# Attention probabilities and a first set of folded weights: their multiplications by VectorE in place of GpSimd

## The chip, the cores and the metric

The kernel runs on one core of a Trainium2 chip. The metric is the device time of one execution in microseconds (us): the median of several runs. The profile describes one execution, instruction by instruction. Engines are TensorE (PE in the profile, its weight loads PEld), VectorE (DVE), ScalarE (ACT), GpSimd (POOL) and SyncE (SP, which issues most of the DMAs).

## The reference, cut to what matters

Two small transformer stacks run one after the other on 512 tokens of width 1024, in float32. The change touches their two self-attentions. The first, with a forget gate, has 16 heads of 64 features and a causal mask; the norm's gain `kv_norm_g` stands ahead of the keys and values:

```
hk = rmsnorm(x, kv_norm_g);  kvf = hk @ kvf_w          # keys, values, gate
q  = rmsnorm(x, norm_mix_g[1]) @ fox_wq
s  = q @ k.T / 8 + (c_q - c_k);  s = where(key <= query, s, -inf)
p  = softmax(s);  out = (p @ v) @ fox_wo
```

The second is a sum of three dilated branches, which the kernel computes as one softmax over 512 keys with a bias table (the number of branches that hold a key, and the relative bias, stand in it), again with 16 heads of 64:

```
q, k, v = split(rms_norm(x, mix_norm[1]) @ w_qkv)
o = softmax(q @ k.T / 8 + bias + log(count)) @ v;  x = x + o @ w_out
```

Around them lie a convolution block, two cross-attentions to 256 memory tokens, two squared-ReLU MLPs, a short convolution and two SwiGLU MLPs.

## The kernel before, in words

All activations lie transposed, 128 features on the partitions and 512 tokens along the row, in 8 tiles. A float32 product is made of three TensorE products of rounded parts: each operand is split into a high part (`whi`, `ahi`; ScalarE rounds it, lines 770, 215) and a remainder (`wlo`, `alo`; VectorE subtracts, lines 773, 216), and `mm3` (line 171) adds high x high, high x remainder and remainder x high into one PSUM bank.

Both attentions run `heads_attention` (line 735). Heads go in pairs, since two heads of 64 fill 128 partitions. For each pair, `KeysQueries` loads the weight columns of its keys and queries into one raw tile; `parts_of` (line 755) cuts them into pieces, and each piece is a chain: `gained` multiplies the raw weights in place by the norm's gain, one factor per row (line 760, in the first attention alone, where three projections with two gains read one activation), `high` rounds them, `low` makes the remainder. These chains are put on a list and issued one step at a time between matmuls (`tick`). Values are projected in four groups of 256 columns (`v_steps`), their weights cut in the same way. In a piece's owner, `owner[1]` is the number of the pair or of the value group, so `owner[1] > 0` leaves out the first pair's keys and queries (four multiplications) and the first group of values (four). The other 40 are given to a function `pinned`.

When a pair's key and query products end, `evac` (line 799) scales them (line 801), ScalarE rounds them (806), and VectorE makes the remainders (808) and a copy (814) that the scores read; GpSimd clears halves of a tile (812).

`scores(head)` (line 939) makes four tiles of scores, one per block of 128 queries; block i has (i + 1) x 128 keys, so the tiles have 512, 384, 128 and 256 columns in the order 3, 2, 0, 1. For each tile VectorE adds the bias and takes the row's extreme (line 967), ScalarE takes the exponential and the row's sum (970), VectorE the reciprocal of the sum (971), and GpSimd multiplies the tile by it (972). In the first attention the bias itself is made by ScalarE (1188) and masked by GpSimd (1191) for up to three tiles of a head ahead of time. `transposed` (line 976) then transposes the four tiles by TensorE (`transpose`, line 93), ten blocks, into PSUM, where they are split in two parts; `values` multiplies them with the values one part of a head later (`pend`).

Between the scores of a head and its transposes, and between those and the next head, other matmuls fill the time of TensorE: the next pair's keys and queries, the values, the output projection. `PLAN`, `PLAN_AHEAD` and `FRACS` say how many. So the tiles of probabilities have a fixed amount of TensorE work in which to become ready.

The order on each engine is made by the framework when the program is built: it simulates the program with costs of its own, and gives an engine that is free in that simulation the earliest line that is ready. TensorE's matmuls, and what goes through `pinned`, keep the order of the program among themselves on their engine. Each engine then executes its list strictly in that order.

Of the kernel before, what the change touches and what calls it, by code (L numbers as in the profile page):

```python
# [13 lines left out]
OP = mybir.AluOpType  # L14
AX = mybir.AxisListType

P = 128
# [63 lines left out]
def model_kernel(tc, a, c_mats, c_onehot, c_lnn, out):  # L81
    nc = tc.nc
# [6 lines left out]
    def matmul(*args, **kw):  # L89
        tc.keep_in_program_order(nc.tensor.matmul(*args, **kw))  # L90
# [4 lines left out]
    def pinned(ins):  # L95
        return tc.keep_in_program_order(ins)
# [20 lines left out]
    def bank(tag="g"):  # L117
        return psum["pool"].tile([P, 512], F32, name="ps_" + tag, tag=tag, bufs=psum["bufs"][tag])
# [616 lines left out]
    def heads_attention(specs, fold, h, nrm, bias_of, hp, wo, prologue, ahead=0):  # L735
# [19 lines left out]
        def parts_of(owner, view, nk, width, f, cuts, pl, tag):  # L755

            w = []

            def gained(v, k0, n):
                ins = nc.gpsimd.tensor_tensor(  # L760
                    v, v, f[:, k0 : k0 + n].unsqueeze(2).to_broadcast([P, n, width]), op=OP.mult
                )
                if owner[1] > 0:
                    pinned(ins)

            def high(v, k0, n):
                if not w:
                    w.append(pl.tile([P, nk, width], F32R, name="whi", tag="whi" + tag, bufs=2))
                    w.append(pl.tile([P, nk, width], F32R, name="wlo", tag="wlo" + tag, bufs=2))
                nc.scalar.copy(w[0][:, k0 : k0 + n, :], v)  # L770

            def low(v, k0, n):
                nc.vector.tensor_tensor(  # L773
                    w[1][:, k0 : k0 + n, :], v, w[0][:, k0 : k0 + n, :].bitcast(F32), op=OP.subtract
                )

            n = nk // cuts
            for k0 in range(0, nk, n):
                v = view[:, k0 : k0 + n, :]
                for fn in (gained, high, low) if f is not None else (high, low):  # L780
                    pieces.append((owner, lambda fn=fn, v=v, k0=k0: fn(v, k0, n)))
            return w
# [148 lines left out]
        def bias_early(head):  # L931

            if head not in biases:
                biases[head] = {}
                bias_fns[head] = bias_of(head)
            i = (3, 2, 0, 1)[len(biases[head])]
            biases[head][i] = bias_fns[head](i)

        def scores(head):
            pair, e = divmod(head, 2)  # L940
            sm = hp.tile([P, NT], F32, name="sm", tag="sm", bufs=3)
            mx = hp.tile([P, NT], F32, name="mx", tag="mx", bufs=3)
            rs = hp.tile([P, NT], F32, name="rs", tag="rs", bufs=3)
            sall = hp.tile([P, 10 * P], F32, name="sall", tag="s", bufs=1)
            pr = [None] * NT
            half = None
            parts = []
            for i in (3, 2, 0, 1):
                n = (i + 1) * P
                if i == 0:  # L950
                    sc = half[:, 3 * P :]
                else:
                    sc = bank("s")
                    if i == 2:
                        half = sc
                    sc = sc[:, 0:n]
                qq = qk[pair][1][0][:, e, i * P : (i + 1) * P]
                matmul(sc, qq, qk[pair][0][0][:, e, 0:n], start=True, stop=False)
                matmul(sc, qq, qk[pair][0][1][:, e, 0:n], start=False, stop=True)
                parts.append((i, sc))  # L960
            for n, (i, sc) in enumerate(parts):
                if n + BIAS_AHEAD < NT:
                    bias_early(head)
                elif head < 15:
                    bias_early(head + 1)
                s = sall[:, P * i * (i + 1) // 2 : P * (i + 1) * (i + 2) // 2]
                nc.vector.tensor_tensor_reduce(
                    s, sc, biases[head][i], 1.0, 3.0e38, op0=OP.add, op1=OP.min, accum_out=mx[:, i : i + 1]
                )
                nc.scalar.activation(s, s, AF.Exp, scale=-1.0, bias=mx[:, i : i + 1], accum_out=sm[:, i : i + 1])  # L970
                nc.vector.reciprocal(rs[:, i : i + 1], sm[:, i : i + 1])  # L971
                pinned(nc.gpsimd.tensor_scalar(s, s, rs[:, i : i + 1], 1.0, op0=OP.mult, op1=OP.mult))  # L972
                pr[i] = s
            return pr

# [79 lines left out]
        for pair in range(8):  # L1055
            n, late = (PLAN_AHEAD if ahead else PLAN)[pair]
            seq = [lambda: stream_run(1)] * (n - late)
            if pair < 7:
                seq = seq + [lambda pair=pair: kq_run(pair + 1, 1)] * 16
            seq = seq + [lambda: stream_run(1)] * late  # L1060
            total = len(seq)
            done = 0
            for e in range(2):
                head = pair * 2 + e
                pr = scores(head)
                fr = (FIRST_FRACS if head == 0 else FRACS) if pair < 7 else LAST_FRACS
                for part in range(3):
                    goal = int(round(total * (e + sum(fr[: part + 1])) / 2))
                    for fn in seq[done:goal]:
                        fn()  # L1070
                    done = goal
                    if part == 0 and pend is not None:
                        values(*pend)
                        pend = None
                    if part == 1:
                        pend = (head, transposed(pr))
# [343 lines left out]
```

## Time and profile before

| | |
|---|---|
| median of 3 runs | 2662.1 us (2660.45 to 2663.39) |
| the profiled execution, and its span | 2659.51 us, 2657.7 us |
| TensorE busy | 2605.3 us, 98% of the span |
| VectorE busy | 1489.1 us, 56% |
| ScalarE busy | 1096.9 us, 41% |
| GpSimd busy | 555.0 us, 21% |
| line 972 on GpSimd, 128 products | 75.9 us, 604 ns on average |
| line 760 on GpSimd, 48 multiplications | 53.9 us, 1147 ns on average |
| mean granted clock of TensorE | 0.994 |

The span is the time from the first to the last instruction; the execution's own time holds some 1.8 us more around it. [...] A wait is listed with the engine that waited and the instruction whose end released it last. In a row of the timeline, brackets hold the idle time of that engine ahead of the instruction; a row without them followed the one before it without idle time.

### The profile page before, as it was taken

The page shows a single profiled execution, that of the slowest core. Times are in us where ns is not written, and L with a number is a line of the kernel's source. Part 1 is how long each engine was busy: PE and PEld are TensorE (multiplying, and loading weights), DVE is VectorE, ACT ScalarE, POOL GpSimd, SP SyncE. Part 2 cuts the span into 40 slices and gives each one's busy share as a digit, 9 for nine tenths or more (in the row PEclk, how much of TensorE's full clock was granted, in tenths as well). Part 3 has the DMA queues.
Part 4 walks back from the last instruction along what each step waited for, and adds up shares of the span by engine and source line. Part 5 has one row for each costly group of instructions (what it writes and reads, how often), then busy time and mean ns, then how long its engine had stood idle before and what let it go on. Part 6 is the DMA issues. An engine that isn't in the chain of part 4 may idle for free.

```text
span 2657.7 us, 32286 instructions
## 1 busy us (share of the span) xinstructions
PE 2605.3 (98%) x12521; PEld 2184.0 (82%) x12521; DVE 1489.1 (56%) x2215; ACT 1096.9 (41%) x1843; POOL 555.0 (21%) x586
## 2 busy tenths in 40 slices
PE   8999999999999999999999999999999999999999
PEld 6889888888878877888888788878888888788888
DVE  6995664443558887554344665343335777643333
ACT  6755443322337665442223323232224666422223
POOL 5862120000226532110000501111112221210111
PEclk9999999999999999999999999999999999999999
DMA  7255133233322322233333233843323323233331
GB/s 211 83 197 181 48 111 95 95 95 95 96 77 68 100 76 72 78 105 103 102 97 95 80 95 97 114 142 102 100 86 111 92 84 90 76 96 99 95 87 56
DMA packets 318057, 264.82 MB, mean 100 GB/s; under 512 B 6741, under 2 KB 304273, under 8 KB 317905
## 3 DMA queue, kind: packets, MB, share of 16 engines
q1 hardware_dynamic: 313808, 252.90, 31.3%
q0 software_dynamic: 1616, 5.52, 1.9%
q10 hardware_dynamic: 2480, 4.33, 0.5%
q8 instruction: 99, 1.62, 0.2%
q14 instruction: 54, 0.43, 0.0%
HBM read 251.16 MB, written 11.57 MB: 99 GB/s over the span
## 4 chain that ended last, share of the span: by engine, by line
PE 56%; DVE 2%; DMA 2%; issue 1%; ACT 1%; POOL 0%; ACTq 0%; DVEq 0%; POOLq 0%
PE ps_g L90 52%; DMA raw<-in_ffn_w_gate 2%; PE ps_s L90 2%; PE ps_t L90 1%; PE ps_t L93 1%; DVE wlo L168 0%; DVE x L1261 0%; DVE alo L228 0%; POOL ssq L252 0%; DVE x L574 0%; ACT ahi L227 0%; DVE x L1259 0%; DVE x L916 0%; ACT sq L248 0%; DVE wlo L773 0%
## 5 line engine op out<-in xcount | busy, mean ns | idle before, releaser
L90 PE MATMUL ps_g<-ahi,whi 128*128 128x512 f32 x3052 | 1196.5, 392 | 9.2 <-DVE x L574 4.9
L90 PE MATMUL ps_g<-ahi,wlo 128*128 128x512 f32 x3052 | 1190.2, 390 | 0.0
L90 PE MATMUL ps_g<-alo,whi 128*128 128x512 f32 x3052 | 1189.7, 390 | 0.0
L167 ACT CAST whi<-raw 128x1024 fp32r<-128x1024 f32 (+2 forms) x384 | 384.1, 1007 | 1115.2 <-PE ps_g L90 1035.3
L90 PEld LDWEIGHTS ps_g<-ahi,whi 128*128 128x128 f32 x3052 | 575.8, 189 | 127.8 <-issue 5.6
L90 PEld LDWEIGHTS ps_g<-ahi,wlo 128*128 128x128 f32 x3052 | 575.2, 188 | 121.7 <-DVE wlo L168 0.8
L90 PEld LDWEIGHTS ps_g<-alo,whi 128*128 128x128 f32 x3052 | 575.8, 189 | 115.4
L168 DVE TENSOR_TENSOR wlo<-raw,whi 128x1024 fp32r<-128x1024 f32 (+2 forms) x384 | 463.8, 1213 | 78.1 <-ACT whi L167 73.4
L574 DVE TENSOR_TENSOR x<-ps_g,x 128x512 f32<-128x512 f32 x144 | 99.2, 689 | 337.5 <-PE ps_g L90 337.4
L252 POOL TENSOR_TENSOR ssq<-ssq,sq 128x512 f32<-128x512 f32 x78 | 121.3, 1556 | 609.0 <-issue 313.7
L718 POOL TENSOR_TENSOR g<-g,rb 128x512 f32<-128x512 f32 x44 | 74.4, 1691 | 566.3 <-ACT g L717 566.3
L684 DVE SCALAR_TENSOR_TENSOR t<-ps_g,rb 128x512 f32<-128x512 f32 x64 | 44.1, 691 | 171.9 <-PE ps_g L90 171.9
L760 POOL TENSOR_TENSOR raw<-raw,gcols 128x512 f32<-128x512 f32 x48 | 53.9, 1147 | 304.3 <-DMA raw<-in_kvf_w 304.3
L414 POOL TENSOR_TENSOR pa<-pa,pr 128x512 f32<-128x512 f32 x80 | 111.8, 1400 | 18.7 <-ACT pa L410 8.2
L722 DVE TENSOR_TENSOR u<-ps_g,g 128x512 f32<-128x512 f32 x44 | 30.4, 691 | 141.9 <-PE ps_g L90 135.7
L406 DVE SCALAR_TENSOR_TENSOR ps_s<-u,gcols,ps_s 128x512 f32<-128x512 f32 x152 | 104.2, 744 | 0.2
L972 POOL TENSOR_SCALAR sall<-sall,rs 128x512 f32<-128x512 f32 (+3 forms) x128 | 75.9, 604 | 129.9 <-DVE rs L971 118.8
L773 DVE TENSOR_TENSOR wlo<-raw,whi 128x512 fp32r<-128x512 f32 x128 | 95.2, 772 | 13.5 <-ACT whi L770 13.4
L770 ACT CAST whi<-raw 128x512 fp32r<-128x512 f32 x128 | 74.1, 620 | 53.5 <-PE ps_g L90 47.4
L715 DVE TENSOR_TENSOR t<-ps_g,rb 128x512 f32<-128x512 f32 x44 | 30.4, 690 | 114.5 <-PE ps_g L90 114.5
L228 DVE SCALAR_TENSOR_TENSOR alo<-x,gcols,ahi 128x512 fp32r<-128x512 f32 x64 | 81.0, 1277 | 13.7 <-ACT ahi L227 13.7
L216 DVE TENSOR_TENSOR alo<-u,ahi 128x512 fp32r<-128x512 f32 x116 | 79.5, 689 | 1.4 <-ACT ahi L215 1.4
(245 smaller groups left out, 2843.7 us busy)
## 6 DMA issues: line engine op xcount, KB each, us to landing
raw<-in_ff_w SPq DMA_DIRECT2D x64, 1024.0 KB, 4.9
raw<-in_ffn_w_gate SPq DMA_DIRECT2D x44, 512.0 KB, 3.9
raw<-in_ffn_w_up SPq DMA_DIRECT2D x44, 512.0 KB, 5.2
raw<-in_ffn_w_down SPq DMA_DIRECT2D x16, 1024.0 KB, 5.1
raw<-in_conv_pw_w SPq DMA_DIRECT2D x16, 512.0 KB, 5.4
raw<-in_mem_wk SPq DMA_DIRECT2D x8, 1024.0 KB, 4.9
raw<-in_mem_wv SPq DMA_DIRECT2D x8, 1024.0 KB, 5.4
raw<-in_mem_wq SPq DMA_DIRECT2D x8, 1024.0 KB, 4.8
```

What stands on the lines that cost most here:

```text
L90: tc.keep_in_program_order(nc.tensor.matmul(*args, **kw))
L167: nc.scalar.copy(hi, view)
L168: nc.vector.tensor_tensor(lo, view, hi.bitcast(F32), op=OP.subtract)
L216: nc.vector.tensor_tensor(lo, src, hi.bitcast(F32), op=OP.subtract)
L228: nc.vector.scalar_tensor_tensor(lo, src, g, hi.bitcast(F32), op0=OP.mult, op1=OP.subtract)
L252: nc.gpsimd.tensor_tensor(self.ssq, self.ssq, dst, op=OP.add)
L406: nc.vector.scalar_tensor_tensor(acc, u[:, j : j + T], tapw(j), acc, op0=OP.mult, op1=OP.add)
L414: nc.gpsimd.tensor_tensor(pa, pa, pr, op=OP.add)
L574: nc.vector.tensor_tensor(x[m], acc, x[m], op=OP.add)
L718: nc.gpsimd.tensor_tensor(g, g, nrm.b, op=OP.mult)
L773: nc.vector.tensor_tensor(w[1][:, k0 : k0 + n, :], v, w[0][:, k0 : k0 + n, :].bitcast(F32), op=OP.subtract)
L972: pinned(nc.gpsimd.tensor_scalar(s, s, rs[:, i : i + 1], 1.0, op0=OP.mult, op1=OP.mult))
```

## The change

Two edits, no other line differs:

```diff
             def gained(v, k0, n):
-                ins = nc.gpsimd.tensor_tensor(
-                    v, v, f[:, k0 : k0 + n].unsqueeze(2).to_broadcast([P, n, width]), op=OP.mult
-                )
+                by = f[:, k0 : k0 + n].unsqueeze(2).to_broadcast([P, n, width])
                 if owner[1] > 0:
-                    pinned(ins)
+                    pinned(nc.gpsimd.tensor_tensor(v, v, by, op=OP.mult))
+                else:
+                    nc.vector.tensor_tensor(v, v, by, op=OP.mult)
...
                 nc.vector.reciprocal(rs[:, i : i + 1], sm[:, i : i + 1])
-                pinned(nc.gpsimd.tensor_scalar(s, s, rs[:, i : i + 1], 1.0, op0=OP.mult, op1=OP.mult))
+                nc.vector.tensor_scalar(s, s, rs[:, i : i + 1], None, op0=OP.mult)
                 pr[i] = s
```

The first edit gives the eight multiplications of the first pair's weights and of the first group of values to VectorE; the 40 others stay on GpSimd, pinned as before. The second gives the 128 products that normalise the probabilities (four a head, 16 heads, two attentions) to VectorE, with one multiplication in place of two (the second was by 1.0), and no longer pinned.

## Rows read from the trace of the kernel before

**Rows 1.** Waits of TensorE, whole span: waited for, us, times, longest.

```profile
PE ps_t L93 <- POOL sall L972: 11.0, 13, 2.4
PE ps_t L90 <- POOL ssq L252: 8.1, 5, 3.0
```

**Rows 2.** Busy us by stretch: PE, PEld, DVE, ACT, POOL; clock, DMA, GB/s.

```profile
790.00:1000.00 210.00, 198.41 (x1100) 170.95 (x1099) 169.69 (x393) 149.42 (x352) 102.62 (x169) 0.98 0.25 78
2065.00:2275.00 210.00, 209.43 (x1207) 182.78 (x1206) 162.30 (x413) 130.63 (x310) 43.80 (x78) 1.00 0.29 85
```

**Rows 3.** Timeline of TensorE, transposes behind a wait: start, us, instruction, idle before.

```profile
791.95 0.33 PE L93 MATMUL ps_t<-mats,sall 128*128 128x128 f32 x1 [1.60 <-POOL sall L972]
...
831.88 0.33 PE L93 MATMUL ps_t<-mats,sall 128*128 128x128 f32 x1 [0.89 <-POOL sall L972]
832.58 1.20 PE L93 MATMUL ps_t<-mats,sall 128*128 128x128 f32 x9 [0.38 <-POOL sall L972]
...
885.76 2.18 PE L93 MATMUL ps_t<-mats,sall 128*128 128x128 f32 x9 [2.42 <-POOL sall L972]
...
984.19 2.12 PE L93 MATMUL ps_t<-mats,sall 128*128 128x128 f32 x9 [1.14 <-POOL sall L972]
```

**Rows 4.** Busy us by stretch behind four stalls; the granted clock is third from last.

```profile
793.00:797.00 4.00, 4.00 (x18) 3.52 (x17) 2.28 (x4) 1.44 (x3) 0.00 (x0) 0.57 0.00 0
886.00:889.00 3.00, 3.00 (x13) 2.76 (x13) 1.29 (x2) 2.30 (x5) 1.71 (x2) 0.55 0.00 0
984.00:988.00 4.00, 3.81 (x14) 3.43 (x15) 1.71 (x3) 1.44 (x3) 0.13 (x1) 0.57 0.02 5
...
831.00:836.00 5.00, 3.75 (x29) 3.53 (x30) 3.54 (x7) 2.75 (x6) 4.98 (x7) 1.00 0.49 201
```

**Rows 5.** Timeline of VectorE in head 3.

```profile
824.38 1.24 DVE L814 CAST qk<-qk 64x512 fp32r<-64x512 f32 x1
...
827.08 0.42 DVE L814 CAST qk<-qk 64x512 fp32r<-64x512 f32 x1
...
828.68 1.27 DVE L773 TENSOR_TENSOR wlo<-raw,whi 128x512 fp32r<-128x512 f32 x2
829.98 1.59 DVE L808 TENSOR_TENSOR qk<-t,qk 64x512 fp32r<-64x512 f32 x2
831.61 0.16 DVE L971 RECIPROCAL rs<-sm 128x1 f32<-128x1 f32 x1
```

**Rows 6.** Timeline of ScalarE in head 3: the last row sum.

```profile
830.58 0.18 ACT L970 ACTIVATION_READ_ACCUMULATOR sall<-sall,mx 128x1 f32 x1
```

**Rows 7.** Timeline of GpSimd in head 3: the last product, and what follows.

```profile
832.05 0.47 POOL L972 TENSOR_SCALAR sall<-sall,rs 128x256 f32<-128x256 f32 x1
832.50 2.04 POOL L760 TENSOR_TENSOR raw<-raw,gcols 128x512 f32<-128x512 f32 x2
```

**Rows 8.** Timeline of VectorE and of GpSimd in head 0.

```profile
791.70 0.16 DVE L971 RECIPROCAL rs<-sm 128x1 f32<-128x1 f32 x1 [0.62 <-ACT sall L970]
...
791.52 0.92 POOL L972 TENSOR_SCALAR sall<-sall,rs 128x128 f32<-128x128 f32 x2
```

**Rows 9.** VectorE's products by a column: count, shortest/median/longest ns, first and last start.

```profile
L1306 DVE TENSOR_SCALAR y<-z,gcols x8: 473/476/1514, 1508.8 to 1617.7; 128x512 f32<-128x512 f32 x8
...
L339 DVE TENSOR_SCALAR xt<-xt,rtm x4: 753/753/753, 6.3 to 11.5; 128x1024 f32<-128x1024 f32 x4
```

**Rows 10.** Timeline: a VectorE product beside a GpSimd addition.

```profile
1474.61 1.51 DVE L1261 TENSOR_SCALAR x<-x,gcols 128x512 f32<-128x512 f32 x1
...
1474.35 1.48 POOL L252 TENSOR_TENSOR ssq<-ssq,sq 128x512 f32<-128x512 f32 x1 [1.95 <-ACT sq L248]
```

**Rows 11.** Timeline of GpSimd and VectorE ahead of the first attention.

```profile
701.49 4.04 POOL L760 TENSOR_TENSOR raw<-raw,gcols 128x512 f32<-128x512 f32 x4 [304.30 <-DMA raw<-in_kvf_w]
...
738.55 8.02 POOL L760 TENSOR_TENSOR raw<-raw,gcols 128x512 f32<-128x512 f32 x8
...
739.48 9.67 DVE L773 TENSOR_TENSOR wlo<-raw,whi 128x512 fp32r<-128x512 f32 x2
```

## The prediction, made before the changed kernel ran

> **What bounds the kernel now.** I read the waits of TensorE first, then busy time by stretch, then the order of time around each stall. TensorE carries the kernel: in all 2657.7 us of the profiled span it waited 11.0 us for GpSimd's normalised probabilities and 8.1 us for GpSimd's sums of squares [rows 1]. The reader is to see that these two waits are the only sizeable ones that GpSimd ends. By stretch, the first attention (heads at 790 to 1000 us, called the forget-gate stage) has TensorE busy 198.41 of 210 us, so 11.6 idle, and VectorE 169.69; the second (2065 to 2275 us, the dilated stage) has TensorE 209.43 of 210 and VectorE 162.30 [rows 2]. So whatever the 128 products of line 972 can give back lies in the first 16 heads; the other 16 stall almost nowhere.
>
> The stalls there: 1.60 us before head 0's transposes, 0.89 and then 0.38 before head 3's, 2.42 in head 7, 1.14 in head 14 [rows 3]; heads 1 and 5 are like head 3. What follows a stall has a price too. Behind the stalls of heads 0, 7 and 14 the granted clock is 0.57, 0.55 and 0.57 of full speed over 4, 3 and 4 us, TensorE being at its lower level (1.2 GHz) for most of it; around head 3's stall it stays at 1.00 [rows 4]. The three falls lose 4 x 0.43 + 3 x 0.45 + 4 x 0.43 = 4.8 us. Stalls and falls together: 11.0 + 4.8 = 15.8 us, the most that the change can win from this wait.
>
> **Is GpSimd what is late?** Head 3 says no. From the first score on, VectorE's rows carry no wait: a cast of 1.24 us at 824.38 and its like of 0.42 at 827.08, two weight remainders from 828.68, two query remainders from 829.98, and only then, at 831.61, the last reciprocal [rows 5]. ScalarE had its row sum ready at 830.58 + 0.18 = 830.76 [rows 6], so the last reciprocal stood 0.85 us behind VectorE's own queue. GpSimd's last product then ran from 832.05 to 832.52 [rows 7], and the transposes ran on at 832.58. The view names GpSimd because its semaphore came last; of the chain it holds only 832.52 - 831.77 = 0.75 us. Heads 1, 5 and 7 have the same order. In head 0 VectorE waits 0.62 us for ScalarE before the last reciprocal, and GpSimd ends at 791.52 + 0.92 = 792.44 [rows 8].
>
> **What the change costs and gives, part by part.**
>
> *One product on VectorE.* The nearest rows are products of one f32 tile by a per-partition column: 128x512 in 473 ns (line 1306, its lowest), 128x1024 in 753 ns (line 339) [rows 9]. The line through both is 193 ns + 0.547 ns a column: 263, 333, 403, 473 ns for the four widths, 1.47 us a head, 23.5 us in each attention. The upper end of one 128x512 product is 1.51 us, where GpSimd was in the middle of an addition [rows 10].
> [...]
>
> *Heads 1, 3, 5 and 7.* If VectorE's order stays, the products of the first three tiles (473 + 403 + 263 = 1.14 us) stand ahead of the last reciprocal, and the last tile takes 0.16 + 0.33 instead of the 832.52 - 831.61 = 0.91 it takes now: 1.14 - 0.42 = +0.72 us a head. That is the upper end without collisions. The lower end is that the whole stall goes, about -1.3 (head 3: 0.89 + 0.38). The planner decides between them: it issues what is ready, in its simulated time, earliest line first. With 1.14 us more ahead of them the two query remainders (829.98) would begin at about 831.1, when the last row sum (830.76) is there; so I expect the last reciprocal and its product to pass at least the second of them. Then the product ends at about 831.1 + 0.69 + 0.08 + 0.33 = 832.2, 0.3 earlier than now. Against it: GpSimd, freed of its products, starts its next weight multiplications, now at 832.50 [rows 7], perhaps 1 us earlier, and they meet this product. I take -0.2 a head, -0.8 in all.
>
> *Head 0.* The reciprocal at 791.70, then 0.16 + 0.33: 792.19 against 792.44, so -0.25 [rows 8]. The clock's fall behind it I leave in. Bounds 0 and -3.3 (the stall and its fall). *Heads 14 and 15:* 0.
>
> *The second attention.* The 23.5 us fall into 210 - 162.3 = 47.7 us of idle VectorE [rows 2], and GpSimd has little else there (43.80 us busy, these products included). Cover: VectorE's idle time between heads. Without it, at the place of each product, the cost is at most a few tenths a head; bounds -0.6 (all idle of TensorE there) and +4. I take 0.
>
> *The eight early multiplications.* GpSimd ran the first four from 701.49 to 705.53 [rows 11]; the other four follow at 714. On VectorE they are 8 x 0.64 = 5.1 us (two inputs in SBUF, like the two weight remainders of 1.27 us [rows 5]), beside TensorE's feed-forward matmuls, which don't read these weights; their accumulators are emptied by VectorE behind at most two or three of the products. What is left on GpSimd are the eight multiplications of the second pair and second values, 738.55 to 746.57: they, not the ones that move, stand ahead of the last sum of squares, hold two VectorE remainders for 9.67 us, and cost a good part of the 8.1 us [rows 1, 11]: the last sum begins at 746.57, not when its square is there. They stay where they are unless the planner's order shifts. Taken 0; bounds -4.6 (a stall of the size of those in heads 0 to 14, 3 us, and a fall of the clock like theirs, 1.6 [rows 3, 4]) and +5.1 (all eight ahead of an accumulator).
>
> No edit issues a DMA or removes one. SP's load of the second values waits until the first pair's raw tile is free, that is until VectorE's remainders of it are done, whichever engine multiplied it; the early edit can move that load by the 2.6 us of four products at most, and the weights that it brings are multiplied only from 738.55 on.
>
> Sum: -0.8 - 0.25 = about -1 us. The profiled execution took 2659.5 us (span 2657.7 and 1.8 around it), the median of the runs 2662.1, so 2.6 more; the forecast is 2658.5 in the profile's terms and 2661 for the median.
>
> **Rivals.**
>
> *A. All the stalls go.* The last reciprocal and product move ahead of the query remainders in all heads, as the second attention, with no multiplications of weights on GpSimd, runs today without stalls. For it: the row sum waits 0.85 us for VectorE in head 3, and a product passes no semaphore to another engine. Against it: VectorE would have 169.7 + 23.5 = 193 us of work in a stretch shrunk to some 195. -11.0 - 4.8 = 2646; half of it, 2654.
>
> *B. VectorE becomes the bound (slower).* Place: heads 1, 3, 5, 7. Price: +0.72 each, 2.9 us; the stalls of 1.27 us (head 3) and its like grow to 2 and more, near what stood before the falls in heads 0 and 7, so three more falls at 1.6 us, 4.8. Collisions with the weight multiplications add up to 1 us a head, as the cast of 1.24 us beside one (its like 0.42, so 0.8 more). +7.7 to +11: 2670 to 2673. It decides from the point where the last reciprocal keeps its place behind the remainders. For it: zero idle time of VectorE in these heads, 81% busy over the stage. Against it: the order is planned anew.
> [...]
>
> *C. Only the early edit works.* GpSimd, rid of the first eight, does the second pair's sooner, and the sum of squares is not held: -4.6, 2657.5.
>
> *D. Nothing moves at all,* since the last product only changes its engine: 2662.
>
> **How the numbers follow.** The forecast's own case, with C and D and small results of both signs, 0.43; A 0.33, in its full or its half form; B 0.24. A measurement of this kernel can tell about 0.2% from no change, 5.3 us, so the line lies at 2656.8 and 2667.4: faster 0.33, same 0.43, slower 0.24. The range 2649 to 2671 leaves out the full form of A and the far end of B, about 2 in 10. The likeliest case alone spans 2657 to 2666.
>
> **What would show it.** Right: TensorE's wait for the probabilities in the first attention, then put down to VectorE, stays between 7 and 12 us; the last product of head 3 ends 0.2 to 0.5 us after where it did, counted from the first score, earlier or later; VectorE's busy time grows by about 24 us in each attention; products of 0.47 us for 512 columns; no GpSimd work on line 972. Wrong: the wait falls below 3 us with the clock at 1.00 throughout (A), or exceeds 14 us with more stretches under 0.8 (B), or the wait for the sums of squares at the start of the stage is gone (C). Stalls in the second attention above 3 us would show that its idle time is no cover.

## The result, and the profile after

The changed kernel took 2680.2 us (median of 4 runs, 2674.7 to 2684.8), the kernel before beside it 2661.6 (4 runs, 2660.5 to 2663.4): ratio 1.0069, 95% interval 1.0056 to 1.0083. It is 18.7 us slower, and the forecast was no change (2661, range 2649 to 2671). The profiled execution took 2679.55 us, its span is 2677.8, 20.1 us more than before.

First the waits of TensorE after (waited for, us, times, longest), which answer to [rows 1]:

```profile
PE ps_t L93 <- DVE sall L972: 21.8, 9, 4.6
PE ps_t L90 <- POOL ssq L252: 7.8, 5, 3.0
PE ps_g L90 <- DVE wlo L773: 1.2, 1, 1.2
```

The wait for the probabilities has a new name and has doubled, from 11.0 us. The wait for the sums of squares has stayed. Busy time by stretch (PE, PEld, DVE, ACT, POOL; clock, DMA, GB/s), for [rows 2]; the second attention begins 17 us later than before:

```profile
790.00:1000.00 210.00, 188.89 (x1029) 164.47 (x1028) 182.38 (x425) 141.87 (x335) 67.88 (x106) 0.94 0.25 74
2082.00:2292.00 210.00, 206.85 (x1196) 180.78 (x1195) 178.12 (x475) 130.35 (x309) 7.30 (x14) 1.00 0.29 82
```

The loss is in the first attention: TensorE idles 21 of these 210 us instead of 11.6, and runs the rest at a mean granted clock of 0.94 of full speed instead of 0.98. From the first transposes of head 0 to those of head 15 the kernel before took 994.96 - 791.95 = 203.0 us, after 1014.27 - 794.14 = 220.1: +17.1 of the 20.1. The same stretch of the second attention grew by 2.8 (192.7 to 195.6); 2.2 come ahead of head 0, and as much is gained back between the two. These 2.2 need not be the change's: prod_second below, which is the kernel before up to this point, reached head 0's transposes at 795.70, later than either.

The stalls ahead of the transposes in heads 0, 1, 3, 5 and 7 (timeline of TensorE: start, us, instruction, idle before), for [rows 3]:

```profile
794.14 0.33 PE L93 MATMUL ps_t<-mats,sall 128*128 128x128 f32 x1 [1.99 <-DVE sall L972]
...
811.72 1.54 PE L93 MATMUL ps_t<-mats,sall 128*128 128x128 f32 x9 [4.47 <-DVE sall L972]
...
841.88 1.20 PE L93 MATMUL ps_t<-mats,sall 128*128 128x128 f32 x9 [2.94 <-DVE sall L972]
...
871.57 2.18 PE L93 MATMUL ps_t<-mats,sall 128*128 128x128 f32 x9 [3.94 <-DVE sall L972]
...
904.40 2.18 PE L93 MATMUL ps_t<-mats,sall 128*128 128x128 f32 x9 [4.56 <-DVE sall L972]
```

Heads 1, 3, 5 and 7 waited 1.41, 1.27, 1.54 and 2.42 us before; now 4.47, 2.94, 3.94 and 4.56, so 9.3 us more. The granted clock about four of these stalls (third from last in each row), for [rows 4]:

```profile
812.00:816.00 4.00, 4.00 (x24) 4.00 (x23) 2.88 (x6) 2.48 (x5) 0.00 (x0) 0.57 0.11 16
842.00:847.00 5.00, 5.00 (x29) 4.95 (x30) 3.84 (x7) 2.61 (x6) 0.00 (x0) 0.66 0.07 11
870.00:874.00 4.00, 2.43 (x12) 2.43 (x13) 3.51 (x7) 1.49 (x3) 0.39 (x1) 0.56 0.01 4
901.00:906.00 5.00, 1.60 (x8) 1.60 (x9) 3.90 (x9) 0.95 (x2) 0.00 (x0) 0.52 0.01 1
```

Head 3 ran on at 1.00 before; now the engine is at its lower level, 0.50 of full speed, for most of the 5 us about that stall too, and about those of heads 1 and 5. At that level matmuls of 512 columns begin 0.43 us apart (kernel before, 794.33 to 796.03), so 1.2 columns a ns (the prediction's 1.2 GHz, if a column takes a cycle); at 1.00 they begin 0.23 us apart (899.82 to 901.19). The stretch from head 0's to head 15's transposes, before and after, holds the same 1071 matmuls:

```profile
791.95:994.96 203.01, 193.45 (x1071) 167.04 (x1072) 164.75 (x383) 144.91 (x341) 100.63 (x163) 0.97 0.26 80
794.14:1014.27 220.13, 198.57 (x1071) 172.74 (x1072) 190.69 (x444) 145.56 (x341) 67.63 (x103) 0.94 0.24 74
```

So of the 17.1 us TensorE idled 12.0 more (9.56 to 21.56) and was busy 5.1 longer with the same work, at the lower mean clock. Most of the idle time is the wait for the probabilities, 20.6 us in this stage against 10.8 (0.2 of the 11.0 lay in the second attention).

Why the stall of head 3 grew is read from its VectorE timeline, for [rows 5]:

```profile
831.03 1.24 DVE L814 CAST qk<-qk 64x512 fp32r<-64x512 f32 x1
...
834.85 0.48 DVE L972 TENSOR_SCALAR sall<-sall,rs 128x512 f32<-128x512 f32 x1
...
835.78 0.42 DVE L972 TENSOR_SCALAR sall<-sall,rs 128x384 f32<-128x384 f32 x1
...
836.30 0.29 DVE L972 TENSOR_SCALAR sall<-sall,rs 128x128 f32<-128x128 f32 x1
836.50 1.38 DVE L773 TENSOR_TENSOR wlo<-raw,whi 128x512 fp32r<-128x512 f32 x2
837.92 2.86 DVE L808 TENSOR_TENSOR qk<-t,qk 64x512 fp32r<-64x512 f32 x2
840.81 0.16 DVE L971 RECIPROCAL rs<-sm 128x1 f32<-128x1 f32 x1
841.01 0.82 DVE L972 TENSOR_SCALAR sall<-sall,rs 128x256 f32<-128x256 f32 x1
```

ScalarE's last row sum there, for [rows 6], and GpSimd, for [rows 7]:

```profile
837.21 0.19 ACT L970 ACTIVATION_READ_ACCUMULATOR sall<-sall,mx 128x1 f32 x1
```

```profile
836.98 0.37 POOL L1191 TENSOR_SCALAR_AFFINE_SELECT dt<-dt 128x128 f32<-128x128 f32 x1 [2.42 <-ACT dt L1188]
837.31 4.37 POOL L762 TENSOR_TENSOR raw<-raw,gcols 128x512 f32<-128x512 f32 x3
```

The row sum is there at 837.40, and the last reciprocal begins at 840.81: it stands 3.4 us behind VectorE's queue, where it was 0.85. Three products are new in that queue. The two query remainders, 1.59 us before, take 2.86, beside three weight multiplications of GpSimd that began at 837.31. Before, these came right behind the last product on GpSimd [rows 7], when the remainders were done. From the first score to the end of the last product, called the head's chain below, the head takes 12.85 us instead of 10.19.

Head 7 shows a second kind of delay, as other subtractions stand between its last reciprocal and its last product:

```profile
902.73 0.16 DVE L971 RECIPROCAL rs<-sm 128x1 f32<-128x1 f32 x1
902.81 0.66 DVE L1009 TENSOR_TENSOR ot<-ps_t,lowp 64x512 f32<-64x512 f32 x1
903.40 0.68 DVE L773 TENSOR_TENSOR wlo<-raw,whi 128x512 fp32r<-128x512 f32 x1
904.00 0.34 DVE L972 TENSOR_SCALAR sall<-sall,rs 128x256 f32<-128x256 f32 x1
```

The planned order puts 1.19 us of them ahead of that product; in head 1 the subtraction of line 1009 stands ahead of the last reciprocal.

Head 0, for [rows 8], and the prices, for [rows 9] (VectorE's rows of lines 972 and 764: count, shortest/median/longest ns, first and last start):

```profile
794.15 0.16 DVE L971 RECIPROCAL rs<-sm 128x1 f32<-128x1 f32 x1
794.35 0.35 DVE L972 TENSOR_SCALAR sall<-sall,rs 128x256 f32<-128x256 f32 x1
```

```profile
L972 DVE TENSOR_SCALAR sall<-sall,rs x128: 266/411/1228, 791.5 to 2285.6; 128x512 f32<-128x512 f32 x32, 128x384 f32<-128x384 f32 x32, 128x128 f32<-128x128 f32 x32, 128x256 f32<-128x256 f32 x32
...
L764 DVE TENSOR_TENSOR raw<-raw,gcols x8: 676/683/721, 701.9 to 717.3; 128x512 f32<-128x512 f32 x8
```

The start of the stage, for [rows 11]: GpSimd and VectorE.

```profile
739.17 8.02 POOL L762 TENSOR_TENSOR raw<-raw,gcols 128x512 f32<-128x512 f32 x8
747.16 1.25 POOL L252 TENSOR_TENSOR ssq<-ssq,sq 128x512 f32<-128x512 f32 x1
...
740.10 9.67 DVE L773 TENSOR_TENSOR wlo<-raw,whi 128x512 fp32r<-128x512 f32 x2
```

The burst of eight and what it holds up are as they were.

### The profile page after: what moved, and what is told of

The parts are those of the page before. It is cut to its first block, busy times and chain, and to the rows that moved or that the text cites. A ratio compares the mean times of both kernels' runs of the same rounds, so it can differ in the third digit from the quotient of the medians.

```text
span 2677.8 us, 32253 instructions
## 1 busy us (share of the span) xinstructions
PE 2611.7 (98%) x12521; PEld 2191.0 (82%) x12521; DVE 1538.1 (57%) x2351; ACT 1097.6 (41%) x1843; POOL 472.5 (18%) x450
## 4 chain that ended last, share of the span: by engine, by line
PE 55%; DVE 3%; DMA 2%; issue 1%; ACT 1%; POOL 0%; ACTq 0%; DVEq 0%; POOLq 0%
PE ps_g L90 51%; DMA raw<-in_ffn_w_gate 2%; PE ps_s L90 2%; PE ps_t L90 1%; PE ps_t L93 1%; DVE wlo L168 1%; DVE x L1261 0%; DVE alo L228 0%; POOL ssq L252 0%; DVE x L574 0%; ACT ahi L227 0%; DVE wlo L773 0%; DVE x L916 0%; DVE x L1259 0%; ACT sq L248 0%
## 5 line engine op out<-in xcount | busy, mean ns | idle before, releaser
L414 POOL TENSOR_TENSOR pa<-pa,pr 128x512 f32<-128x512 f32 x80 | 111.5, 1397 | 18.7 <-ACT pa L410 8.2
L90 PE MATMUL ps_g<-whi,ahi 128*128 128x256 f32 x256 | 75.5, 295 | 0.3 <-DVE t L801 0.3
L90 PE MATMUL ps_g<-wlo,ahi 128*128 128x256 f32 x256 | 74.6, 291 | 1.2 <-DVE wlo L773 1.2
```

What stands on the lines that cost most here:

```text
L414: nc.gpsimd.tensor_tensor(pa, pa, pr, op=OP.add)
```

## The experiments

The theories, as the expectations name them. **Q**: the products stand ahead of the last reciprocal on VectorE, and GpSimd's weight multiplications, no longer held behind products on their own engine, collide with VectorE's two-input operations. **L**: the early edit is the cost. **V**: VectorE's load itself, wherever the products stand. **O**: the order on VectorE alone. **G**: the hop to GpSimd and back is what costs. Each kernel was timed beside the kernel before on the same chip, whose median was 2660.6 to 2661.8 us there; a ratio carries its 95% interval, and 0.001 is 2.7 us.

**early_only: the first edit without the second** (line 972 as before).

```diff
-                ins = nc.gpsimd.tensor_tensor(v, v, f[...], op=OP.mult)
+                by = f[...]
                 if owner[1] > 0:
-                    pinned(ins)
+                    pinned(nc.gpsimd.tensor_tensor(v, v, by, op=OP.mult))
+                else:
+                    nc.vector.tensor_tensor(v, v, by, op=OP.mult)
```

> The early edit alone (eight multiplications of the first pair's weights and first values on VectorE; the 128 products of line 972 stay on GpSimd). Theory Q (the loss sits in the first attention, where the products lengthen VectorE's queue ahead of the last reciprocal and GpSimd, rid of them, starts its weight multiplications into that same queue): within 2 us of before. Rival L (the early edit delays the start of the stage): +2 to +5 us, and the wait for the sums of squares at 748 us grows.

Measured 2661.1 us, ratio 0.9999 [0.9991, 1.0008]. TensorE's wait for the sums of squares is 8.0 us. The early edit costs and gives nothing; L falls.

**prod_first and prod_second: the products of one attention alone.**

```diff
-                pinned(nc.gpsimd.tensor_scalar(s, s, rs[:, i : i + 1], 1.0, ...))
+                if fold is not None:      # prod_second: fold is None
+                    nc.vector.tensor_scalar(s, s, rs[:, i : i + 1], None, op0=OP.mult)
+                else:
+                    pinned(nc.gpsimd.tensor_scalar(s, s, rs[:, i : i + 1], 1.0, ...))
```

> The products of the first attention alone on VectorE, those of the second and the eight early multiplications on GpSimd as before. Theory Q: +14 to +18 us, stalls of 3 to 4.5 us in heads 1, 3, 5 and 7. Rival V (VectorE's additional 23.5 us of work cost the same in both attentions): half of the whole loss, +9.

> The products of the second attention alone on VectorE. Theory Q: +2 to +4 us (stalls before the transposes of three heads, where before there were hardly any). Rival V: +9.

prod_first: 2677.0, ratio 1.0058 [1.0044, 1.0072], with stalls of 4.62, 2.94, 3.94 and 4.55 us in heads 1, 3, 5 and 7. prod_second: 2664.9, ratio 1.0010 [1.0001, 1.0019]; TensorE waits 1.1 us for VectorE's products in all. 64 products on VectorE cost 15.4 us by the ratio in the one attention and 2.7 in the other (16.4 and 4.3 by the medians). The load is the same in both, so it isn't what decides; the weight multiplications on GpSimd, which only the first has, may be.

**hold: the changed kernel, with GpSimd held back.** Behind each product of the first attention GpSimd copies one column of it, pinned, so that its weight multiplications keep the place that the products gave them. The products stay on VectorE.

```diff
                 nc.vector.tensor_scalar(s, s, rs[:, i : i + 1], None, op0=OP.mult)
+                if fold is not None:
+                    pinned(nc.gpsimd.tensor_scalar(held[:, i : i + 1], s[:, 0:1], 1.0, 1.0, ...))
```

> The changed kernel, with one tiny GpSimd copy of a 128x1 column of each tile behind its product in the first attention, pinned, so that GpSimd's weight multiplications stay behind the last product as they did before the change; VectorE's work is the same as in the changed kernel. Theory Q: the query remainders of heads 1, 3, 5 and 7 take 1.4 to 1.6 us again in place of 2.9, the last product 0.34 in place of 0.8; stalls shrink by about 1.5 us each and some falls of the clock go: 6 to 10 us faster than the changed kernel, some 2669 to 2674. Rival V: within 2 us of the changed kernel.

Measured 2672.2, ratio 1.0038 [1.0025, 1.0051]. Head 3, VectorE, then GpSimd. Each experiment has line numbers of its own: here the product is line 973, in others 974, 982 or 983, the reciprocal is the line ahead of it, and the query remainders are 808, 810 or 816.

```profile
836.23 1.28 DVE L773 TENSOR_TENSOR wlo<-raw,whi 128x512 fp32r<-128x512 f32 x2
837.55 1.40 DVE L808 TENSOR_TENSOR qk<-t,qk 64x512 fp32r<-64x512 f32 x2
838.98 0.16 DVE L972 RECIPROCAL rs<-sm 128x1 f32<-128x1 f32 x1
839.18 0.35 DVE L973 TENSOR_SCALAR sall<-sall,rs 128x256 f32<-128x256 f32 x1
```

```profile
839.62 0.19 POOL L975 TENSOR_SCALAR held<-sall 128x1 f32<-128x1 f32 x1 [1.96 <-DVE sall L973]
839.77 3.04 POOL L762 TENSOR_TENSOR raw<-raw,gcols 128x512 f32<-128x512 f32 x3
```

The same VectorE instructions in the same order, with these three weight multiplications behind them instead of beside them: the remainders take 1.40 instead of 2.86, the last product 0.35 instead of 0.82, the head's chain 10.83 instead of 12.85. So 2.0 us of this head's 2.66 were the collision, and 0.64 the queue. The three weight multiplications lost as well: 4.37 us beside the remainders and the product, 3.04 behind them. That is 1.01 us each, the pace of the burst of eight above (8.02). So the two hinder each other, with 1.46 us lost on one side and 1.33 on the other; by what means, the traces don't show.

Head 3 isn't the whole. The chains of heads 1, 3, 5 and 7 took 10.18, 10.19, 10.08 and 11.15 us before, 13.00, 12.85, 12.27 and 14.34 in the changed kernel, and take 12.24, 10.83, 10.73 and 12.49 here: holding takes back 6.2 of the 10.9 us that they had grown by. In time it gives back 8.0 of the 18.7 us, so Q's range is met, V's (within 2 us) isn't, and the collisions that hold prevents are not all of the loss. In heads 1 and 7 the subtraction behind the remainders (line 1012 here) still stands ahead of the last product, and in head 1 a cast took 2.41 us instead of 1.24.

**order, order_hold: the last reciprocal and product ahead of the query remainders**, without and with GpSimd held back.

```diff
+                    # line 808, m == 1: issued behind the latest product
+                    ins = nc.vector.tensor_tensor(dst, t[own, :], hi[own, e, :]..., op=OP.subtract)
+                    if m:
+                        behind_product(ins)   # an edge of order, no wait
```

> The changed kernel with one edge of order on VectorE: the query remainders (line 808, queries) stand behind the latest product, so that in heads 1, 3, 5 and 7 the last reciprocal and product come ahead of them. GpSimd is still free to start its weight multiplications early. Theory Q (queue and collision together): the remainders' 1.4 us plus their collision leave the chain, but the product itself can still meet a weight multiplication: 6 to 10 us faster than the changed kernel, 2669 to 2674. Rival O (order alone is the cause): back at before, 2661, within 2 us.

> Both: the edge of order, and GpSimd held behind each product by a tiny copy of a 128x1 column. Theory Q: the collision and the remainders are both gone, only the three products ahead of the last reciprocal are left: 2660 to 2666. Rival V (VectorE's load itself): 2670 or more.

order: 2673.0, ratio 1.0049 [1.0035, 1.0063]. order_hold: 2666.4, ratio 1.0024 [1.0014, 1.0035], 0.4 us above its range. Head 3 of order, and its two waits:

```profile
833.45 0.94 DVE L982 TENSOR_SCALAR sall<-sall,rs 128x256 f32<-128x256 f32 x1
834.42 2.86 DVE L816 TENSOR_TENSOR qk<-t,qk 64x512 fp32r<-64x512 f32 x2
837.32 0.68 DVE L1019 TENSOR_TENSOR ot<-ps_t,lowp 64x512 f32<-64x512 f32 x1
```

```profile
PE ps_t L93 <- DVE sall L982: 11.9, 10, 2.1
...
PE ps_t L93 <- DVE ot L1019: 5.2, 5, 1.9
```

The wait for the probabilities is back near its old size, but the collision (2.86) is still there, now behind the product, and falls on the subtraction behind it (line 1019), for which TensorE newly waits 5.2 us. With GpSimd held too, the first wait is 9.8 and the second 3.3 us. Order alone gives back 7.2 of the 18.7 us, holding 8.0, both together 13.8; O falls as a sole cause.

**before_no_mult and after_no_mult: neither kernel with the 40 weight multiplications of GpSimd.**

```diff
             def gained(v, k0, n):
+                if owner[1] > 0:
+                    return
```

> The kernel before with the 40 weight multiplications of GpSimd (second pair and second values on) left out, so the weights of these pairs lack the norm's gain: the other half of the pair of kernels in which nothing on GpSimd can collide with VectorE's two-input operations. The order on VectorE is planned anew: the last reciprocal of heads 1, 3, 5, 7 now stands ahead of the query remainders. Theory Q (queue ahead of the last reciprocal, and GpSimd's freed multiplications colliding): a good part of the 11.0 us and of the 8.1 us waits go, and the falls behind them: 2644 to 2655. Theory V (VectorE's own load): says nothing of this kernel alone. Rival G (the hop to GpSimd and back is the price): the wait for GpSimd's products stays 8 us or more, 2655 to 2660.

> The changed kernel with the same 40 multiplications left out. Here too the last reciprocal and product of heads 1, 3, 5, 7 stand ahead of the query remainders, so both parts of the price are taken away at once. Theory Q: within 3 us of the kernel before without them (2642 to 2658), where with them the change costs 18.7. Theory V: the 128 products are still on VectorE, so the difference of the two stays at 10 us or more. Rival G: faster than its counterpart by 5 us or more, since the product no longer goes to another engine.

Measured 2647.4 (ratio 0.9944 [0.9931, 0.9958]) and 2649.6 (0.9953 [0.9941, 0.9966]). The change, worth 18.7 us with these multiplications, costs 2.2 us without them, about its part in the second attention (2.7) and near the noise of these runs. V and G fall. The kernel before itself gains 14.3 us, the changed one 30.6: the multiplications cost something before as well, as the cast of 1.24 us showed [rows 5]. Head 3 of after_no_mult:

```profile
821.78 1.29 DVE L775 TENSOR_TENSOR wlo<-raw,whi 128x512 fp32r<-128x512 f32 x2
822.98 0.15 DVE L973 RECIPROCAL rs<-sm 128x1 f32<-128x1 f32 x1
823.17 0.35 DVE L974 TENSOR_SCALAR sall<-sall,rs 128x256 f32<-128x256 f32 x1
823.55 1.40 DVE L810 TENSOR_TENSOR qk<-t,qk 64x512 fp32r<-64x512 f32 x2
```

All 128 products are on VectorE, and the head stalls 0.71 us only, for the subtraction behind the remainders. The planned order is also another one: the last product precedes the query remainders. So this pair takes both parts of Q away at once; it doesn't weigh them, which hold and order do.

**last_only: only the last tile's product (256 columns) on VectorE.** Nothing then stands ahead of the last reciprocal, and the last hop between engines is gone.

```diff
+                if i == 1:
+                    nc.vector.tensor_scalar(s, s, rs[:, i : i + 1], None, op0=OP.mult)
+                else:
                     pinned(nc.gpsimd.tensor_scalar(s, s, rs[:, i : i + 1], 1.0, ...))
```

> The kernel before with the last tile's product alone (256 columns, one of four per head) on VectorE, the other three on GpSimd: nothing is added to VectorE's queue ahead of the last reciprocal, and GpSimd is held as before up to the third product. Theory Q: chains of heads 1, 3, 5 and 7 within 0.5 us of before, unless the last product meets a weight multiplication (up to 1 us): 2658 to 2666. Rival V: a quarter of the loss, +4 to +5.

Measured 2660.4, ratio 0.9999 [0.9991, 1.0008]. TensorE waits 5.9 us for GpSimd's products and 5.5 for VectorE's, in all what it was. The stalls of heads 3 and 5 shrink to 0.89 and 1.17; those of heads 1 and 7 grow to 2.90 and 2.97. In head 1 the product took 1.08 us beside a weight multiplication, and in head 7 the subtraction of line 1012 stands ahead of it. So gains and losses cancel: the time is in Q's range and V's +4 to +5 falls, but the run does not price the hop by itself.

**before_order and before_order_w: the kernel before, with the query remainders behind the latest reciprocal;** in the second the weight remainders (line 773) too.

```diff
+                latest[:] = [nc.vector.reciprocal(rs[:, i : i + 1], sm[:, i : i + 1])]
...
+                    if m:
+                        behind_product(ins)   # query remainders
+                behind_product(ins)           # before_order_w alone: weight remainders
```

> The kernel before (products on GpSimd) with the same edge of order: the query remainders stand behind the latest reciprocal. In head 3 the row sum waited 0.85 us for VectorE. Theory Q: the stalls of heads 1, 3, 5 and 7 shrink by 0.5 to 1.4 us each and that of head 7 loses its fall of the clock: 2655 to 2659, faster than both kernels. Rival G (GpSimd's hop and product are what is late): within 1 us of before.

> The kernel before with the query remainders and also the weight remainders of VectorE ordered behind the latest reciprocal: a try at a version faster than the one with the query remainders alone (ratio 0.9990). Theory Q: the last reciprocal of head 3 moves ahead by up to the 1.27 us of two weight remainders, stalls of heads 1, 3, 5, 7 go below 1 us each: 2651 to 2658. The other way: the remainders that wait come too late for the projections that read them, and TensorE's wait for them grows by 3 us or more: 2659 to 2668.

before_order: 2657.7, ratio 0.9990 [0.9981, 0.9998]. It is the fastest version that computes the whole, faster than both kernels, by a margin at the edge of what these runs can tell. Its wait, and head 3's last reciprocal:

```profile
PE ps_t L93 <- POOL sall L982: 8.9, 12, 1.4
```

```profile
829.45 0.16 DVE L981 RECIPROCAL rs<-sm 128x1 f32<-128x1 f32 x1 [0.82 <-ACT sall L980]
```

Now the reciprocal waits 0.82 us for ScalarE: the queue on VectorE is out of the way there, and the next limit is the row sum. The time was met by another way than expected: the stalls of heads 1, 3, 5 and 7 are 2.03, 1.08, 1.35 and 1.44 us, where each was to shrink by 0.5 to 1.4, so only head 7's did. Over the stage TensorE idles 9.2 us instead of 9.6 and is busy 2.0 us less; the clock is 1.00 about head 7's stall (882 to 888 us), where it was 0.72 (884 to 890). before_order_w: 2667.6, ratio 1.0023 [1.0014, 1.0032], slower. The time is in the range of its second case, by another wait than expected:

```profile
PE ps_t L93 <- POOL sall L983: 11.7, 12, 2.7
...
PE ps_t L93 <- DVE ot L1020: 7.4, 5, 1.7
```

TensorE never waited 3 us for the weight remainders. In head 3 one of the two and the query remainders now stand behind the last reciprocal, the query remainders at 2.31 us beside GpSimd's multiplications, and TensorE waits 1.71 or 1.72 us for the subtraction of line 1020 behind them in each of heads 1, 3, 5 and 7, where it waited 0.27 in before_order.

## Why the prediction was wrong, point by point

**What bounds the kernel, and where the stalls are: right.** The loss, like the gain hoped for, lies in the first 16 heads, above all 1, 3, 5 and 7, and VectorE's own queue was what came late there.

**The failed step: "I take -0.2 a head" for heads 1, 3, 5 and 7.** Two things went wrong in it. It expected the planner to put the last reciprocal and product ahead of the second query remainder. It didn't: in the timeline of head 3 both remainders (837.92) still stand ahead of the reciprocal (840.81). And it let GpSimd's freed multiplications meet only the last product; the upper end of +0.72 was named "without collisions", and these came in rival B alone, at up to 1 us a head. In head 3 the chain grew by 2.66 us. The products ahead of the last reciprocal are 1.17 of it, against 1.14 predicted. Less 0.36 for the last reciprocal and product had they run clear (0.55 instead of 0.91; 0.42 was predicted), the queue's part is +0.81; hold measured 0.64, and the prediction's upper end was 0.72. The collisions in head 3 are the other 1.85: 1.27 in the query remainders, 0.47 in the last product, 0.11 in the weight remainders. In heads 1 and 7 the chains stay 2.06 and 1.34 us above before even with GpSimd held, as the subtraction behind the remainders was planned ahead of the last product there and, in head 1, the cast grew; the sum had no term for such a change of order. The text saw the cause, GpSimd starting its multiplications earlier (perhaps 1 us; in head 3 it was 1.8, counted from the first score), and sized it by one cast [rows 5]. It did not follow the pinned order through: what held these multiplications behind the remainders was the products themselves.

**Rival B was the mechanism, and too small.** It decides "from the point where the last reciprocal keeps its place behind the remainders", and that is the case. Its 2670 to 2673 had 0.72 and up to 1 us a head, and three falls of the clock at 1.6 us. Measured were 9.3 us more of stalls in the four heads, and a clock of 0.94 in the stage. The 4.8 us for the clock are near the 5.1 by which TensorE's busy time grew; the stalls were what it had too small. The sign that the text named for B, a wait above 14 us with more stretches under 0.8, came. Its title, VectorE as the bound, is not what the runs show: with all 128 products on VectorE and no weight multiplications beside them, the change costs 2.2 us.

**The price of a product: right.** 0.48, 0.42, 0.35 and 0.29 us for the four widths, against 0.47, 0.40, 0.33 and 0.26.

**Head 0: right in its chain.** From the first score to the last product 5.42 us instead of 5.61, so -0.19 against -0.25. The stall grew by 0.46 all the same, as the first bias came 0.63 us later against TensorE's last matmul. That is not shown to be the change's: prod_second, the same as the kernel before up to there, stalls 1.95 and 0.22 us in head 0, where the kernel before stalls 1.60 and 0.21.

**Heads 14 and 15: near 0.** Their stalls went from 1.94 us to 2.44, and from 0.42 to none.

**The second attention: inside its bounds.** Taken 0, bounds -0.6 to +4; prod_second measured +2.7 (0.3 to 5). The idle time of VectorE was not a full cover: waits of 1.1 us for a product, 1.0 for a reciprocal and 0.8 for the subtraction of line 1012 are new there.

**The early edit: right.** Eight products of 0.68 us, where 0.64 was taken, and 0.9999 [0.9991, 1.0008]. Rival C falls with it, as the burst of eight multiplications (739.17) stayed.

**Rival A** fell in the changed kernel: its condition, the last product ahead of the remainders, was not met. Where it was met (order, order_hold), the stalls shrank and did not go.

**What stays open.** order_hold still costs 0.24%. The second attention explains about 0.10; the rest is some 4 us. In the first attention (784 to 1005 us) TensorE's waits are 4.1 us longer than before: 8.7 for the probabilities, less than the 10.8 before, but 2.5 for the subtraction behind the remainders and 2.2 for a weight remainder, which are new, and 2.2 instead of 0.7 for line 926 (916 before). No run takes these apart. The split of the 17.1 us into 12.0 of idle and 5.1 of busy time is that of two profiled executions; no run isolates what one fall of the clock costs.

## What to carry to other kernels

Work that is moved off an engine releases whatever was ordered behind it there (here GpSimd's weight multiplications, 1.8 us earlier in head 3): read the queue of the engine that is relieved as closely as that of the one that is loaded, and ask beside what its next work will then run. A product of 0.35 us is not the price of a move if it was also what kept a 3 us burst of two-input work away from another engine's critical subtractions. Before moving work to an engine, see who is late: where the late instruction stands behind that engine's own queue, reordering the queue is the cheaper try (here 0.9990 against 1.0069), though it too can cost (before_order_w, 1.0023).

## What the runs showed of the hardware that was not expected

A pair of VectorE subtractions of 64x512 took 1.40 us alone and 2.86 beside three GpSimd multiplications of 128x512, and these 4.37 instead of 3.04: both sides lose, and the 1.33 us that the multiplications lose are near the whole of the subtractions' own time. It is not always so: beside the burst of eight, which kept its pace of 1.00 us each, two weight remainders took 9.67 us [rows 11], against 1.27 in head 3 of the kernel before. What decides between the two no run shows. A VectorE product by a column, with a single large input, suffers too: 0.35 us alone and 0.82 or 0.94 there, up to 1.23 for the longest of the 128.
